# Cross attention of a decoder trunk: queries of two heads at a time by seven block products, with key and value tiles ahead of the probabilities in memory

## The chip, the cores and the metric

One core of a Trainium2 chip. The metric is the device time of one execution in microseconds; the time before is the median of three runs, and one execution was also taken by the hardware profiler. The engines are TensorE (PE in the profile, with its weight loads apart as PEld), VectorE (DVE), ScalarE (ACT), GpSimd (POOL) and SyncE (SP). SP issues the plain loads, POOL the loads that add to what is already there.

## The reference

Two decoder layers over 512 tokens of width 1024. Each layer is a half-step feed-forward, a token mixer (differential attention in layer 0, a pooling mixer in layer 1), cross attention to 256 memory tokens, and a second half-step feed-forward; after each stands a layer norm of the scaled sum. The change lies in the cross attention:

```python
def memory_cross_attention(x, mem, wq, wkv, wo):
    q = (x @ wq).reshape(B, S, XA_HEADS, XA_HEAD_DIM)
    k, v = jnp.split(mem @ wkv, 2, axis=-1)
    ...
    s = jnp.einsum('bshd,bmhd->bhsm', q, k).astype(jnp.float32) * (XA_HEAD_DIM ** -0.5)
    p = jax.nn.softmax(s, axis=-1).astype(v.dtype)
    o = jnp.einsum('bhsm,bmhd->bshd', p, v).reshape(B, S, D_MODEL)
    return o @ wo
```

## The kernel before

Every product is kept near float32 by splitting both factors into a high part (a cast to fp32r by ACT, line 120) and a low part (the rest, subtracted by DVE, line 121) and adding three matmuls, high by high, high by low and low by high (`mm3`, lines 205 to 207). Weights come from memory as raw tiles, and each 128x1024 block is split into the tiles `wh` and `wl`. The tokens stand in four tiles `X`; PE turns them (`pt`), and ACT and DVE split the turned blocks into `xh` and `xl` (`turn`).

The feed-forward stages already use seven block products in place of eight (a 2x2 scheme of blocks: the rows of X in two halves of 256 tokens, the weights in two halves of rows and of columns). `second_factors` makes the sums of token blocks that the scheme needs, and `up` loads weight blocks, adds further blocks onto them with POOL DMAs (`more`), and runs the products into three banks `x`, `y` and `z`. Cross attention does not use this before the change: `xa_main` takes each head's keys (`pk`, 48 matmuls of 256 columns), its values (`pv`, 48), and its queries (`xq`, 48 matmuls of 512 columns; for the first head of layer 1 in 96 of 256). Beside that, `weave` lets `xa_side` put in a piece of side work each time the main work has gained a set credit (2500): scores `xs`, softmax, turned probabilities, outputs `xo`. `to_tokens` then multiplies by wo and adds to X. In layer 1 the keys and values of the first two heads and the keys of the third run beside the pooling mixer (`early_kv`). Query, key and value weights are loaded in tiles of 1 MB for a head, two such raw tiles being there, and the splits use five `wh` and five `wl` tiles.

A scheduling layer writes one fixed order for each engine ahead of the run, and an engine takes its instructions in that order: an instruction that waits holds up all behind it on the same engine.

Of the kernel before, what the change touches and what calls it, by code (L numbers as in the profile page):

```python
# [9 lines left out]
F32 = mybir.dt.float32  # L10
# [7 lines left out]
P = 128  # L18
# [26 lines left out]
GATES = {"xa": (1, 2)}  # L45

# [63 lines left out]
class Trunk:  # L110
    def __init__(self, tc, a, out, upto=8):
        self.tc, self.nc, self.a, self.out, self.upto = tc, tc.nc, a, out, upto
        self.side, self.late, self.gates = [], [], []
        self.ln_next_gb, self.kv_bufs = None, 8
# [95 lines left out]
    def weave(self, main, side, gap, lead=0):  # L210
# [3 lines left out]
        for ns in main:  # L214
            self.clock += ns
# [44 lines left out]

    def raw_heads(self, w, c0):
# [21 lines left out]
    def wide(self, raw):  # L283

        got = []
        for j in range(0, 8, 4):
            t = self.hl([P, 4, 256])
            self.split_weights(t[0], t[1], raw[:, j : j + 4])
            got += [(t[0][:, i], t[1][:, i]) for i in range(4)]
        return got  # L290

    def rows(self, w, k0, kn, c0, homes=None):


        got = []
        for k in range(0, kn, 4):
            n = min(4, kn - k)
            raw = self.raw_tile((4, S))
            r0 = (k0 + k) * P
            self.nc.sync.dma_start(  # L300
                raw[:, :n], w[r0 : r0 + n * P, c0 : c0 + S].rearrange("(k p) n -> p k n", p=P)
            )
            if homes:
                got += [home() for home in homes]
                for j, t in enumerate(got):
# [151 lines left out]
    def turn(self, t, half, tag="px"):  # L457
# [6 lines left out]
        if self.ln_next == "ffn":  # L464
# [544 lines left out]
    def da_values(self, h, vs):  # L1009

        raw = self.raw_cols(self.a["da_w_qkv"][0], 2 * D + h * P)
        ws = self.wide(raw)
# [232 lines left out]
    def pool_mixer(self, layer, ln):  # L1245
# [37 lines left out]
        wg = self.wide(self.pool_w)  # L1283
        self.begin_ln(layer, ln, 1.0)
        for t in range(NT):
# [16 lines left out]
            self.turn_late()  # L1302
# [33 lines left out]
    def xa_kv(self, w, h):  # L1336
        kt = self.keys.pop(0) if self.keys else (yield from self.xa_k(w, h))
        return kt, (yield from self.xa_v(w, h))

    def xa_k(self, w, h, raw=None, then=None, turn=True):  # L1340
        rk = raw or self.raw_cols(w, h * 256)
        ps = self.mm("pk").rearrange("p (c n) -> p c n", c=2)
        for j in range(2):
            with self.after(self.x_split if raw and not then else ()):
                wk = self.cols(rk, j)
            if then and j == 1:
                then()
            for k in range(KC):
                yield self.mm3(
                    ps[:, j], (wk[0][:, k], wk[1][:, k]), self.memT[k], k == 0, k == KC - 1  # L1350
                )
        kt = self.kv_tiles((P, 2, MEM))
        if turn:
            self.turn_late()
# [8 lines left out]
    def xa_v(self, w, h, raw=None):  # L1363
        wv = self.wide(raw or self.raw_cols(w, D + h * 256))
# [10 lines left out]
    def xa_head(self, qs, kt, v):  # L1375
# [34 lines left out]
        for c in range(2):  # L1410
# [4 lines left out]
            o = self.pair("oT")  # L1415
            self.split(o[0], o[1], po)
            self.oT.append(o)
            yield

    def early_kv(self, layer, ln, heads, raws):  # L1420
        w, keys = self.a["xa_wkv"][layer], {}

        def load_more():
            keys[1] = self.raw_cols(w, 256)
# [7 lines left out]
        self.keys.append((yield from self.xa_k(w, heads, turn=False)))  # L1432
# [191 lines left out]
```

## Time and profile before

| | us |
|---|---|
| median of three runs | 1936.6 |
| lowest and highest run | 1935.6, 1938.74 |
| the profiled execution | 1932.35 |
| span of its trace | 1930.6 |
| cross attention, layer 0 (about) | 590 to 752 |
| cross attention, layer 1 (about) | 1460 to 1605 |

The span runs from the first to the last instruction of the profiled execution; the execution's own time lies 1.75 us above it and the median 4.25 above that. A line of the timeline gives the start, the duration, the engine, the line of the program, and what is written from what; in square brackets stands the idle time of the engine ahead of it and what ended it. A line of the table of stretches gives the stretch, its length, and the busy time with instruction count of PE, PEld, DVE, ACT and POOL, then the granted TensorE clock (1 is full), the share of the DMA engines, and GB/s. The groups of a tile give the number of instructions with minimum, median and maximum duration in ns, and the first and last start. The DMA list gives the number of loads, the size of each, and the median us from issue to landing.

### The profile page before, as it was taken

The numbers are of one execution on the slowest core, as the hardware profiler recorded it, in microseconds if no ns is written. First come the engines' busy times: TensorE is split into PE (matmuls) and PEld (weight loads), VectorE is DVE, ScalarE is ACT, GpSimd is POOL, SyncE is SP. The second block draws the span as 40 slices with busy tenths as digits, with TensorE's granted clock in tenths as the row PEclk, the third lists the DMA queues.
The fourth block names the chain that finished last, engine by engine and source line by source line (L and its number), as shares of the span: only waits on it lengthen the run. The fifth ranks groups of instructions, "written<-read, shape, count | busy, mean of one in ns | idle before, by whom it ended". The sixth has DMA issues, their size and how long they took to land.

```text
span 1930.6 us, 32520 instructions
## 1 busy us (share of the span) xinstructions
PE 1902.1 (99%) x13114; PEld 1740.5 (90%) x13114; DVE 1566.3 (81%) x2200; ACT 1022.2 (53%) x1580; POOL 315.0 (16%) x276
## 2 busy tenths in 40 slices
PE   8999999999999999999999999999999999999998
PEld 8999998888778888999998999999889889999997
DVE  7888889888867557888888988898887568988886
ACT  6555454567655435655554655455445436555553
POOL 2112121111210001211210321112040012111210
PEclk9999999999999999999999999999999999999999
DMA  9978772322134316977686587778244356867861
GB/s 239 220 169 182 175 138 77 90 80 74 48 117 142 110 66 186 186 175 164 139 194 179 104 179 168 177 162 185 89 153 134 115 140 120 181 158 170 183 133 56
DMA packets 246743, 277.96 MB, mean 144 GB/s; under 512 B 8256, under 2 KB 212544, under 8 KB 246592
## 3 DMA queue, kind: packets, MB, share of 16 engines
q0 software_dynamic: 92928, 92.29, 31.1%
q1 hardware_dynamic: 153664, 183.59, 29.2%
q8 instruction: 103, 1.69, 0.3%
q14 instruction: 48, 0.39, 0.1%
HBM read 273.75 MB, written 2.10 MB: 143 GB/s over the span
## 4 chain that ended last, share of the span: by engine, by line
PE 80%; DVE 12%; ACT 3%; DMA 2%; issue 2%; POOL 1%; SPq 1%; DVEq 0%; ACTq 0%; POOLq 0%
PE x L205 7%; PE x L206 7%; PE x L207 7%; PE z L206 4%; PE z L205 4%; PE z L207 4%; PE ps L205 4%; PE ps L207 4%; PE ps L206 4%; PE px L205 2%; PE px L207 2%; PE px L206 2%; DVE wl L121 2%; PE y L207 2%; PE x L681 2%
## 5 line engine op out<-in xcount | busy, mean ns | idle before, releaser
L666 POOL DMA_DIRECT2D ra<-in_ffn_w_in_dram x132 | 170.3, 1309 | 993.5 <-DVE wl L121 815.2
L120 ACT CAST wh<-ra 128x1024 fp32r<-128x1024 f32 x184 | 193.7, 1053 | 218.9 <-PE x L206 67.5
L121 DVE TENSOR_TENSOR wl<-ra,wh 128x1024 fp32r<-128x1024 f32 x184 | 223.8, 1220 | 73.0 <-ACT wh L120 72.5
L120 ACT CAST wh<-rc 128x1024 fp32r<-128x1024 f32 x136 | 143.1, 1053 | 118.6 <-PE x L206 43.1
L205 PE MATMUL x<-xe,wh 128*128 128x256 f32 x704 | 195.0, 277 | 0.0
L206 PE MATMUL x<-xe,wh 128*128 128x256 f32 x704 | 194.8, 277 | 0.0
L207 PE MATMUL x<-xe,wl 128*128 128x256 f32 x704 | 194.8, 277 | 0.0
L121 DVE TENSOR_TENSOR wl<-rc,wh 128x1024 fp32r<-128x1024 f32 x136 | 164.6, 1219 | 28.4 <-ACT wh L120 28.1
L120 ACT CAST wh<-b 128x1024 fp32r<-128x1024 f32 x112 | 117.8, 1052 | 131.3 <-PE x L206 67.7
L121 DVE TENSOR_TENSOR wl<-b,wh 128x1024 fp32r<-128x1024 f32 x112 | 136.7, 1220 | 40.2 <-ACT wh L120 40.2
L205 PE MATMUL x<-xh,wh 128*128 128x256 f32 x544 | 151.1, 278 | 0.0
L206 PE MATMUL x<-xl,wh 128*128 128x256 f32 x544 | 150.6, 277 | 0.0
L207 PE MATMUL x<-xh,wl 128*128 128x256 f32 x544 | 150.6, 277 | 0.0
L206 PEld LDWEIGHTS x<-xe,wh 128*128 128x128 f32 x704 | 132.5, 188 | 1.4
L205 PEld LDWEIGHTS x<-xe,wh 128*128 128x128 f32 x704 | 132.1, 188 | 1.3
L207 PEld LDWEIGHTS x<-xe,wl 128*128 128x128 f32 x704 | 132.2, 188 | 0.0
L121 DVE TENSOR_TENSOR wl<-raw,wh 128x1024 fp32r<-128x1024 f32 x64 | 81.8, 1285 | 38.8 <-ACT wh L120 38.2
L206 PEld LDWEIGHTS x<-xl,wh 128*128 128x128 f32 x544 | 102.5, 188 | 0.7
L205 PEld LDWEIGHTS x<-xh,wh 128*128 128x128 f32 x544 | 102.1, 188 | 0.7
L207 PEld LDWEIGHTS x<-xh,wl 128*128 128x128 f32 x544 | 102.1, 188 | 0.0
L207 PE MATMUL y<-xh,wl 128*128 128x256 f32 x352 | 98.4, 280 | 1.2
L206 PE MATMUL z<-xl,wh 128*128 128x256 f32 x352 | 97.5, 277 | 0.7 <-DVE xl L121 0.7
(429 smaller groups left out, 6291.6 us busy)
## 6 DMA issues: line engine op xcount, KB each, us to landing
ra<-in_ffn_w_in_dram POOLq DMA_DIRECT2D x132, 512.0 KB, 6.7
rc<-in_ffn_w_in_dram SPq DMA_DIRECT2D x88, 512.0 KB, 5.8
b<-in_ffn_w_out_dram SPq DMA_DIRECT2D x76, 512.0 KB, 4.8
ra<-in_ffn_w_in_dram SPq DMA_DIRECT2D x44, 512.0 KB, 5.4
rc<-in_ffn_w_in_dram POOLq DMA_DIRECT2D x44, 512.0 KB, 6.7
raw<-in_xa_wkv_dram SPq DMA_DIRECT2D x16, 1024.0 KB, 5.4
raw<-in_da_w_qkv_dram SPq DMA_DIRECT2D x16, 512.0 KB, 5.2
raw<-in_xa_wq_dram SPq DMA_DIRECT2D x8, 1024.0 KB, 4.9
```

Source lines behind the costliest of these rows:

```text
L120: self.nc.scalar.copy(hi, src),
L121: self.nc.vector.tensor_sub(lo, src, hi.bitcast(F32)),
L205: mm(out, w[0], x[0], start=start, stop=False, skip_group_check=again)
L206: mm(out, w[0], x[1], start=False, stop=False, skip_group_check=again)
L207: self.last_mm = mm(out, w[1], x[0], start=False, stop=stop, skip_group_check=again)
L666: nc.gpsimd.dma_start(t, source(*block), accum_op=ALU.add)
L681: self.last_mm = nc.tensor.matmul(ps[:, j], v[i][:, k, j * P : (j + 1) * P], x[l][:, k], start=n == i == l == 0, stop=n == 7 and i == 1, s ...
```

## The change

`xa_queries` takes the queries of two heads at once, 512 columns of wq, as seven block products of 24 matmuls with 256 columns each, in the order 0, 1, 3, 6, 4, 5, 2 of the scheme. Three of the seven weight operands are plain blocks, four are sums: four POOL DMAs per pair of heads add a block onto a raw tile once that tile's earlier contents have been split (`more`), sixteen in all. `xa_factors` makes the token sums: s1, a11, a12, s2, s4, s3 on DVE, and the splits of parts 3, 2, 6, 4 and 5 on ACT and DVE, from the turned tokens 2 and 3 after the layer norm. A table, `XA_ORDER`, sets the order of the pieces in each layer: a digit is a piece of that head's keys and values, `s` a step of the factors, `q` and `r` one product of the first and second pair of heads, `Q` and `R` the place from which the side work may use that pair. The side work now comes at a credit of 2100. The fourth weight block (`rd`) is loaded only after the third product's weights are split. Key, value and wo weights are loaded in halves of 512 KB into raw tiles of half the size (five in layer 0, four in layer 1), the `wh` and `wl` tiles become four, the key and value tiles lie in a pool ahead of the probabilities, and the pooling mixer no longer turns the last tokens itself.

```diff
+XA_ORDER = ("0000s00ss" "qq1q11qq1q11qQ" "r222r2r22rr3rrR33333", "qsqs2qsq2sq3qqQ" "r2r3rr33rrrR33")
...
+    def raw_quarter(self, w, r0, c0, width):
+        raw = self.raw_tile((4 * 256 // width, width))
+        rows = w[r0 : r0 + P * 4 * 256 // width, c0 : c0 + width]
+        self.last_load = self.nc.sync.dma_start(raw, rows.rearrange("(k p) n -> p k n", p=P))
+        return raw
+    def raw_keys(self, w, h):
+        return [self.raw_quarter(w, 0, h * 256 + j * P, P) for j in range(2)]
+    def raw_values(self, w, h):
+        return [self.raw_quarter(w, r, D + h * 256, 256) for r in (0, S)]
...
-        if self.ln_next == "ffn":
+        if self.ln_next != "da":
...
-            self.turn_late()
+            if t < NT - 1:
+                self.turn_late()
...
-    def xa_kv(self, w, h):
-        kt = self.keys.pop(0) if self.keys else (yield from self.xa_k(w, h))
-        return kt, (yield from self.xa_v(w, h))
-    def xa_k(self, w, h, raw=None, then=None, turn=True):
-        rk = raw or self.raw_cols(w, h * 256)
+    def xa_kv(self, w, h, turn=None):
+        kt = self.keys.pop(0) if self.keys else None
+        if not kt:
+            kt = yield from self.xa_k(w, h, turn=turn)
+            yield None
...
-            o = self.pair("oT")
-            self.split(o[0], o[1], po)
-            self.oT.append(o)
+            if c == 0:
+                o = self.pair("oT" if len(self.oT) < 4 else "xe", (P, 2, S))
+            self.split(o[0][:, c], o[1][:, c], po)
+            self.oT.append((o[0][:, c], o[1][:, c]))
...
+    def xa_factors(self):
+        nc, F, H = self.nc, self.factors, 2 * P
+        a11, a12, a21, s1 = (self.tmp("oT", (P, 4, H)) for i in range(4))
+        def part(i, x, o=slice(0, H)):
+            self.split(F[i][0][:, :, o], F[i][1][:, :, o], x)
+        for t in (2, 3):
+            o = slice(t % 2 * P, (t % 2 + 1) * P)
+            pts = []
+            for half in range(2):
+                pt = self.aux("pt", ("py", "yz")[half]).rearrange("p (c n) -> p c n", c=4)
+                c0 = half * S
+                with self.behind():
+                    self.transpose4(pt, [self.X[t][:, c0 + j * P : c0 + (j + 1) * P] for j in range(4)])
+                pts.append(pt)
+            nc.scalar.copy(a21[:, :, o], pts[0])
+            nc.vector.tensor_tensor(s1[:, :, o], pts[1], a21[:, :, o], ALU.subtract)
+            part(3, s1[:, :, o], o)
+            part(2, pts[1], o)
+            yield
+        for r, (hi, lo) in zip((a11, a12), F):
+            nc.vector.tensor_tensor(r, hi.bitcast(F32), lo.bitcast(F32), ALU.add)
+        s2, s4, s3 = s1, a12, a21
+        nc.vector.scalar_tensor_tensor(s2, s1, -1.0, a11, ALU.mult, ALU.subtract)
+        nc.vector.scalar_tensor_tensor(s4, s2, -1.0, a12, ALU.mult, ALU.subtract)
+        part(6, s4)
+        yield
+        part(4, s2)
+        nc.vector.tensor_tensor(s3, a11, a21, ALU.subtract)
+        part(5, s3)
+        yield
+    def xa_queries(self, w, h, q):
+        nc, H = self.nc, 2 * P
+        def source(row, col):
+            c0 = (h + col - 1) * H
+            return w[(row - 1) * S : row * S, c0 : c0 + H].rearrange("(k p) n -> p k n", p=P)
+        def load(*block):
+            t = self.raw_tile((4, H))
+            nc.sync.dma_start(t, source(*block))
+            return t
+        def more(t, *block):
+            nc.gpsimd.dma_start(t, source(*block), accum_op=ALU.add)
+        def operand(raw):
+            v = self.hl([P, 4, H])
+            self.split_weights(v[0], v[1], raw)
+            return v
+        def product(ps, v, a, start=False):
+            x = self.factors[a]
+            for j in range(2):
+                o = slice(j * P, (j + 1) * P)
+                for k in range(4):
+                    yield self.mm3(
+                        ps[:, j], (v[0][:, k, o], v[1][:, k, o]), (x[0][:, k], x[1][:, k]),
+                        start and j == k == 0, j == 1 and k == 3, True,
+                    )
+        bank = lambda t: t.rearrange("p (j n) -> p j n", j=2)
+        halves = slice(0, H), slice(H, S)
+        scale = (D // XA_H) ** -0.5
+        def done(i, half, src, by):
+            hi, lo = (t[:, :, halves[half]] for t in q[i])
+            self.split_scaled(hi, lo, src, by)
+        ra = load(1, 1)
+        x = bank(self.aux("x", "px"))
+        v = operand(ra)
+        more(ra, 1, 2)
+        rc = load(2, 1)
+        yield from product(x, v, 0, True)
+        p1 = self.tmp("p", (P, 2, H))
+        nc.scalar.copy(p1, x)
+        yield None
+        y = bank(self.aux("y", "yz"))
+        v = operand(rc)
+        yield from product(y, v, 1, True)
+        nc.vector.tensor_tensor(p1, y, p1, ALU.add)
+        q[0] = self.pair("q", (P, 2, S))
+        done(0, 0, p1, scale)
+        yield None
+        z = bank(self.aux("z", "yz"))
+        v = operand(ra)
+        rd = load(2, 2)
+        more(ra, 2, 2)
+        yield from product(z, v, 3, True)
+        p5 = self.tmp("p", (P, 2, H))
+        nc.scalar.copy(p5, z)
+        yield None
+        v = operand(rd)
+        more(rd, 1, 2)
+        yield from product(z, v, 6)
+        yield None
+        v = operand(ra)
+        more(ra, 2, 1)
+        yield from product(x, v, 4)
+        u2 = self.tmp("p", (P, 2, H))
+        q[1] = self.pair("q", (P, 2, S))
+        nc.scalar.copy(u2, x)
+        nc.vector.tensor_tensor(u2, z, u2, ALU.add)
+        done(1, 0, u2, -scale)
+        yield None
+        yield from product(x, operand(rd), 5)
+        nc.vector.tensor_tensor(p5, x, p5, ALU.add)
+        done(1, 1, p5, -scale)
+        yield None
+        yield from product(x, operand(ra), 2)
...
+        done(0, 1, x, scale)
...
-        early = len(self.kv)
-        for h in range(XA_H):
-            if h >= len(self.kv):
-                self.kv.append((yield from self.xa_kv(wkv, h)))
-            kt, v = self.kv[h]
-            raw = self.raw_cols(wq, h * 256)
-            qs = []
-            ws = [self.cols(raw, c) for c in range(2)]
-            ps = [self.mm("xq") for c in range(2)]
-            for p in ((0, 2 * P), (2 * P, S)) if self.late else ((0, S),):
-                for c in range(2):
-                    yield from self.project(ps[c], ws[c], (p,))
-                    self.turn_late(max(len(self.late) - 1, 0) if c == 0 else 0)
-            for c in range(2):
-                q = self.pair("q")
-                self.split_scaled(q[0], q[1], ps[c], (D // XA_H) ** -0.5)
-                qs.append(q)
-            self.heads.append((self.clock, (qs, kt, v)))
-            if 0 < early and h + early < XA_H:
-                self.kv.append((yield from self.xa_kv(wkv, h + early)))
+        self.late, second = [], self.xa_factors()
+        qs = [[None] * 2 for n in range(2)]
+        works = {n: self.xa_queries(wq, 2 * i, qs[i]) for i, n in enumerate("qr")}
+        works.update((str(h), self.xa_kv(wkv, h)) for h in range(1, XA_H))
+        works["0"] = self.xa_kv(wkv, 0, lambda: next(second))
+        for n in XA_ORDER[layer]:
+            if n == "s":
+                next(second)
+            elif n in "QR":
+                i = "QR".index(n)
+                for j in range(2):
+                    q = [(qs[i][j][0][:, c], qs[i][j][1][:, c]) for c in range(2)]
+                    self.heads.append((self.clock, 2 * i + j, q))
+            else:
+                yield from self.part(works[n])
...
-        bufs = dict(q=8, oT=10, gb=2)
+        bufs = dict(xe=6, q=4, oT=4)
+        self.raw_rows = 2
         if layer == 0:
             self.kv, self.keys = [], []
             mem = self.side_pool("mem")
-            with self.other_pools():
+            with self.stage_pools(4, dict(raw=5), ("wh", "wl", "raw", "kv")):
                 self.stage["mem"] = mem
-                with self.phase_pool(("gb", "gb"), "p", pT=6, p=4, kv=8, _x=0, **bufs):
-                    self.kvp = self.phase["kv"]
+                with self.phase_pool(("xe", "xe"), "p", p=4, pT=4, _x=0, **bufs):
+                    self.kvp = self.stage["kv"]
                     with self.tc.high_priority():
                         self.load_memory("p")
                     self.xa(layer, ln)
             self.close_side()
         else:
-            with self.later, self.phase_pool(("gb", "gb"), "p", _x=0, pT=6, p=4, **bufs):
+            with self.later, self.phase_pool(("xe", "xe"), "p", _x=0, pT=4, p=4, **bufs):
                 self.xa(layer, ln)
     def xa(self, layer, ln):
-        self.heads, self.oT = [], []
-        self.weave(self.xa_main(layer), self.xa_side(), 2500)
+        self.heads, self.oT, self.factors = [], [], self.factor_tiles()
+        self.weave(self.xa_main(layer), self.xa_side(), 2100)
...
-            self.later.enter_context(self.other_pools(("wh", "wl", "mem", "raw")))
+            self.later.enter_context(self.stage_pools(4, dict(raw=4), ("wh", "wl", "mem", "raw")))
```

Where the instructions now stand is shown at two places. The first is DVE at the start of cross attention in layer 0, before the change, from the last step of the layer norm (line 380) to the first head's weights (`xl` low part of the turned tokens, `wl` of weights, `kv` of keys or values):

```order
L380 SCALAR_TENSOR_TENSOR X_77<-X_77,rstd,v 128x1024
L121 TENSOR_TENSOR xl<-pt,xh 128x4x128 x2
L121 TENSOR_TENSOR kv<-pk,kv 128x512
L121 TENSOR_TENSOR xl<-pt,xh 128x4x128 x2
L121 TENSOR_TENSOR wl<-raw,wh 128x1024 x4
L121 TENSOR_TENSOR kv<-pv,kv 128x512
L121 TENSOR_TENSOR wl<-raw,wh 128x1024 x2
L126 SCALAR_TENSOR_TENSOR q<-xq,q 128x512
```

and after it, from the first wide sum, a11, on (`oT` are the tiles that hold the sums s1, a11, a12, s2, s3, s4; lines 1479 to 1491 are `xa_factors`; `wl_6988` is the second product's weight block):

```order
L1484 TENSOR_TENSOR oT_6836<-xh_6439,xl_6441 128x1024
L124 TENSOR_TENSOR xl_6442<-oT_6839,xh_6440 128x4x128
L124 TENSOR_TENSOR xl_6442<-pt_6845,xh_6440 128x4x128
L1479 TENSOR_TENSOR oT_6839<-pt_6900,oT_6838 128x4x128
L1484 TENSOR_TENSOR oT_6837<-xh_6439,xl_6441 128x1024
L124 TENSOR_TENSOR xl_6442<-oT_6839,xh_6440 128x4x128
L124 TENSOR_TENSOR xl_6442<-pt_6900,xh_6440 128x4x128
L124 TENSOR_TENSOR kv_6936<-pv_6870,kv_6935 128x512
L1486 SCALAR_TENSOR_TENSOR oT_6839<-oT_6839,oT_6836 128x1024
L1491 TENSOR_TENSOR oT_6838<-oT_6836,oT_6838 128x1024
L1487 SCALAR_TENSOR_TENSOR oT_6837<-oT_6839,oT_6837 128x1024
L124 TENSOR_TENSOR wl_6988<-raw_6958,wh_6987 128x1024
```

The second product's weights stand behind the build of the sums, and the two steps just ahead of these rows are a narrow sum and a key split.

The second place is ACT at the start of cross attention in layer 1, before the change, from the last turned tokens of the early part (`xh`) to the second head's values:

```order
L120 CAST xh_15929<-pt_16177 128x4x128
L120 CAST xh_15930<-pt_16184 128x4x128
L375 ACTIVATE var_16192<-var_16192 128x1
L120 CAST kv_16229<-pk_16096 128x512
L120 CAST wh_16395<-raw_16389 128x1024
L120 CAST xh_15929<-pt_16295 128x4x128
L120 CAST xh_15930<-pt_16302 128x4x128
L120 CAST wh_16481<-raw_16479 128x1024
L125 ACTIVATE q_16381<-xq_16269 128x512
L120 CAST wh_16485<-raw_16479 128x1024
```

and after it, from the cast of the first summed block to that of the next key weights (`raw_16486` and `raw_16634` are the query weight blocks that POOL adds onto, `raw_16763` key weights; `p_16520` holds the first product, `p_16661` the third):

```order
L123 CAST wh_16630<-raw_16486 128x1024
L1543 COPY p_16520<-x_16488 128x512
L123 CAST xh_16163<-oT_16525 128x4x128
L123 CAST xh_16163<-pt_16531 128x4x128
L123 CAST wh_16669<-raw_16634 128x1024
L1478 COPY oT_16524<-pt_16576 128x4x128
L128 ACTIVATE q_16572<-p_16520 128x2x256
L123 CAST xh_16163<-oT_16525 128x4x128
L123 CAST xh_16163<-pt_16581 128x4x128
L1558 COPY p_16661<-z_16629 128x512
L123 CAST wh_16727<-raw_16486 128x1024
L123 CAST wh_16768<-raw_16763 128x1024
```

Casts of summed weight blocks (`wh_16630`, `wh_16727`) now stand ahead of the copy of the first product, of casts of turned tokens, of key weights and of the factors. On POOL the DMAs that add the blocks stand in the same queue as the layer norm's last step there:

```order
L393 TENSOR_TENSOR rstd_16278<-var_16277,mhalf_82 128x1
L393 TENSOR_TENSOR rstd_16358<-var_16357,mhalf_82 128x1
L1511 DMA raw_16486<-in_xa_wq_dram 128x4x256
L393 TENSOR_TENSOR rstd_16414<-var_16413,mhalf_82 128x1
L1511 DMA raw_16486<-in_xa_wq_dram 128x4x256
L1511 DMA raw_16634<-in_xa_wq_dram 128x4x256
L1511 DMA raw_16486<-in_xa_wq_dram 128x4x256
```

The first of them stands ahead of the last tokens' `rstd`, where before the change POOL had no DMA in this stage.

More of the change, by code (lines that the diff above doesn't have):

```diff
@@ L214, in weave @@
         for ns in main:
+            ns = ns or 0
             self.clock += ns
@@ L285, in wide @@
         got = []
-        for j in range(0, 8, 4):
+        for half in raw:
             t = self.hl([P, 4, 256])
-            self.split_weights(t[0], t[1], raw[:, j : j + 4])
+            self.split_weights(t[0], t[1], half)
             got += [(t[0][:, i], t[1][:, i]) for i in range(4)]
@@ L1011, in da_values @@
         raw = self.raw_cols(self.a["da_w_qkv"][0], 2 * D + h * P)
-        ws = self.wide(raw)
+        ws = self.wide([raw[:, :4], raw[:, 4:]])
         for t in range(0, NT, 2):
@@ L1282, in pool_mixer @@
             yield
-        wg = self.wide(self.pool_w)
+        wg = self.wide([self.pool_w[:, :4], self.pool_w[:, 4:]])
         self.begin_ln(layer, ln, 1.0)
@@ L1363, in xa_v @@
     def xa_v(self, w, h, raw=None):
-        wv = self.wide(raw or self.raw_cols(w, D + h * 256))
+        wv = self.wide(raw or self.raw_values(w, h))
         ps = self.mm("pv").rearrange("p (m n) -> p m n", m=2)
@@ L1431, in early_kv @@
             self.kv.append((kt, (yield from self.xa_v(w, h, raws[1] if h == 0 else None))))
-        self.keys.append((yield from self.xa_k(w, heads, turn=False)))
+        self.keys.append((yield from self.xa_k(w, heads)))
+    def xa_factors(self):
[28 more added lines that the diff above has]
+        yield
```

43 lines of the change are left out of this document (28 added, 15 removed).

## The prediction

> **What bounds the kernel now.** I read the page first (busy shares and the chain that ended last), then the groups of the query products, the timeline of single matmuls, a table of stretches of the two cross-attention stages, and last the rows of VectorE (DVE), ScalarE (ACT) and the DMAs at the start of each stage.
>
> ```profile
> PE 1902.1 (99%) x13114; PEld 1740.5 (90%) x13114; DVE 1566.3 (81%) x2200; ACT 1022.2 (53%) x1580; POOL 315.0 (16%) x276
> PE 80%; DVE 12%; ACT 3%; DMA 2%; issue 2%; POOL 1%; SPq 1%; DVEq 0%; ACTq 0%; POOLq 0%
> ```
>
> TensorE (PE) is busy 99% of the span and carries 80% of the chain. A matmul taken away is a gain only as long as nothing makes PE wait; a wait put in is lost whole. DVE is at 81%, so the second question is where DVE has room.
>
> ```profile
> 590.00:610.00 20.00, 19.59 (x142) 17.94 (x143) 17.22 (x22) 10.24 (x17) 1.08 (x1) 1.00 0.54 167
> 610.00:630.00 20.00, 20.00 (x150) 18.77 (x149) 10.70 (x16) 9.59 (x17) 0.00 (x0) 1.00 0.56 175
> 690.00:710.00 20.00, 20.00 (x95) 16.51 (x94) 9.13 (x15) 6.05 (x12) 0.00 (x0) 1.00 0.29 103
> 1460.00:1480.00 20.00, 19.02 (x162) 18.33 (x161) 16.85 (x21) 11.38 (x18) 1.83 (x2) 1.00 0.58 189
> 1480.00:1500.00 20.00, 20.00 (x120) 17.39 (x119) 10.54 (x19) 10.60 (x21) 0.00 (x0) 1.00 0.47 155
> ```
>
> The columns are PE, its weight loads, DVE, ACT, POOL, granted clock, DMA share and GB/s, for the start and the inside of cross attention in layer 0 (from 590 us) and layer 1 (from 1460 us). Inside a stage PE is full and DVE works 9 to 11 of 20 us: there is room. In the first 20 us of either stage DVE already works 17, with the last layer norm, the splits of X and the first weights.
>
> **What is removed.** The query products leave and seven block products per two heads come.
>
> ```profile
> L205 PE MATMUL xq<-xh,wh x144: 276/394/507, 605.0 to 1543.3; 128*128 128x512 f32 x112, 128*128 128x256 f32 x32
> L206 PE MATMUL xq<-xl,wh x144: 276/394/400, 605.3 to 1543.6; 128*128 128x512 f32 x112, 128*128 128x256 f32 x32
> L207 PE MATMUL xq<-xh,wl x144: 276/394/400, 605.5 to 1543.9; 128*128 128x512 f32 x112, 128*128 128x256 f32 x32
> ```
>
> That is 336 matmuls of 512 columns and 96 of 256 (head 0 of layer 1 runs in halves). The durations overlap, so the price is the distance from start to start:
>
> ```profile
> 1519.62 0.39 PE L207 MATMUL xq<-xh,wl 128*128 128x512 f32 x1
> 1519.85 0.39 PE L205 MATMUL xq<-xh,wh 128*128 128x512 f32 x1
> ...
> 1464.55 0.28 PE L205 MATMUL xq<-xh,wh 128*128 128x256 f32 x1
> 1464.66 0.28 PE L206 MATMUL xq<-xl,wh 128*128 128x256 f32 x1
> 1464.77 0.28 PE L207 MATMUL xq<-xh,wl 128*128 128x256 f32 x1
> ```
>
> 0.233 us (the mean over longer runs of such rows) for 512 columns, 0.113 for 256. Before: 336 x 0.233 + 96 x 0.113 = 89.1 us. After: four pairs of heads x 7 products x 24 = 672 matmuls of 256 columns, 75.9 us. PE gains 13.2 us, 6.8 in layer 0 and 6.4 in layer 1, if it never waits. This is arithmetic on measured distances; I leave it no error.
>
> The Trainium skill (TensorE: Matmul & The Clock Gate, section "Wait — 56ns, not 53.3ns?") speaks against so much: start to start is the columns at 2.4 GHz plus a fixed 2.5 ns, 216 and 109 ns here, by which the smaller tiles would save only 9.6 us. The trace's 0.233 and 0.113 differ from it, and here 512 columns cost a little over twice 256; the trace is used.
>
> **What is added.** Six more weight splits a layer (14 blocks of 128x1024 for queries instead of 8), and the factor build: the sums s1 to s4, a11 and a12 and the splits of parts 3, 2, 6, 4, 5. From the rows
>
> ```profile
> 597.88 1.28 DVE L380 SCALAR_TENSOR_TENSOR X<-X,rstd,v 128x1024 f32<-128x1024 f32 x1
> 599.08 1.28 DVE L121 TENSOR_TENSOR xl<-pt,xh 128x512 fp32r<-128x512 f32 x2
> 600.28 0.68 DVE L121 TENSOR_TENSOR kv<-pk,kv 128x512 fp32r<-128x512 f32 x1
> 602.76 1.29 DVE L121 TENSOR_TENSOR xl<-pt,xh 128x512 fp32r<-128x512 f32 x2 [1.80 <-ACT xh L120]
> 603.97 4.62 DVE L121 TENSOR_TENSOR wl<-raw,wh 128x1024 fp32r<-128x1024 f32 x4
> ```
>
> one 128x512 step takes 0.60 us of DVE's time (599.08 to 600.28 for two) and one 128x1024 step 1.14 ((4.62 - 1.22) / 3). On DVE the six splits are 6.8 us. The build's eight wide steps (a11, a12, s2, s4, s3 and three splits) take 9.1 and its six narrow ones 3.6, against 2.4 for the four narrow splits it replaces: 10.3. With the six narrow adds and subtractions that combine the products (3.6) that is some 21 us a layer. Over a stage of 150 us at half load it vanishes; the rows at 690 show where. It does not vanish at the start, where it is bunched.
>
> *Layer 0.* The first product's weight block is split right after the last X row (done 600.2), so its matmuls can start near 605 as before. After that DVE does in order: six narrow steps of the build, two of key and value, five wide sums, then the second product's weights. 8 x 0.60 + 5 x 1.14 + 1.14 = 11.6 us, so these are ready at 611.8. PE has 24 matmuls (2.7 us) and six that need no low part (0.7), from 605.0: it arrives at 608.4 and waits 3.4 us. The third product's weights come behind three more factor splits, another 1.2. The rest of the chain costs 0 to 1.2. Together 4.6 to 5.8, of which I take 5.0. The order on DVE is fixed beforehand, so nothing can be drawn ahead into these waits; the low end is the first wait alone, 3.4, with key products covering the rest.
>
> *Layer 1.* Here ACT is the trap. Weight blocks are summed by POOL's accumulating DMAs in place, and each may be issued only when the split of the earlier contents is done.
>
> ```profile
> 1462.95 1.22 DVE L247 TENSOR_TENSOR wl<-raw,wh 128x1024 fp32r<-128x1024 f32 x1
> 1464.08 1.28 DVE L378 SCALAR_TENSOR_TENSOR X<-X,mean,gb 128x1024 f32<-128x1024 f32 x1
> 1466.48 1.27 DVE L380 SCALAR_TENSOR_TENSOR X<-X,rstd,gb 128x1024 f32<-128x1024 f32 x1
> ...
> 602.15 1.07 ACT L120 CAST xh<-pt 128x512 fp32r<-128x512 f32 x2
> 603.11 2.96 ACT L120 CAST wh<-raw 128x1024 fp32r<-128x1024 f32 x3
> ...
> ra<-in_ffn_w_in_dram POOLq DMA_DIRECT2D x132, 512.0 KB, 6.7
> raw<-in_xa_wq_dram SPq DMA_DIRECT2D x8, 1024.0 KB, 4.9
> ```
>
> The feed-forward stage's accumulating load of the same 512 KB lands 6.7 us after its issue; a plain load (here of twice the size) takes 4.9, the lower bound. The first split ends near 1464.2, so the summed block is there at 1470.9 (1469.1). In ACT's order its cast stands ahead of the copy of the first product, four casts of X and a weight cast. Behind it: cast 0.95, copy 0.5, two casts of X 1.0; then on DVE the last low part, the addition and the low part of the value weights, 0.6 + 0.6 + 1.14, with small waits between them: 1475.7. PE, with the first two products (48 matmuls), 13 matmuls of values and eight transposes to do from about 1465.1, stands at those value weights from 1472.6: 3.1 us lost (1.3 at the lower bound). The next accumulated block is released at 1478.1 and lands at 1484.8; behind its cast stand a key weight cast (ready 1486.8) and the casts of parts 6 and 4. PE arrives at the keys at 1483.2: 3.6 us (1.8), then about 2.0 more for the two parts. With 0.9 before the first product, 0.7 before the third and 0 to 3.5 where products reuse the x bank, the sum is 10.3 to 13.8. From it go the waits that the old start has, of which the first stands here, with an SP issue that is used further down:
>
> ```profile
> 1463.17 0.41 PE L489 MATMUL pt<-ident,X 128*128 128x128 f32 x2 [0.51 <-DVE X L380]
> ...
> 1469.51 0.38 SPq L233 DMA_DIRECT2D raw<-in_xa_wq_dram  x1
> ```
>
> From start to start this one costs 0.67 and one 4 us later 0.63, 1.3 us together (PE busy 19.02 of 20 in the stretch from 1460). At the lower bound of the DMA: 5.4. I take 9, with ends 5.4 and 12.5.
>
> *Clock.* The one long wait near this stage is followed by a slow stretch:
>
> ```profile
> 1434.02 0.28 PE L205 MATMUL ps<-wh,pooled 128*128 128x256 f32 x1
> 1437.42 0.58 PE L206 MATMUL ps<-wl,pooled 128*128 128x256 f32 x1 [3.11 <-DVE wl L121]
> ...
> 1437.40:1441.00 3.60, 3.58 (x17) 3.58 (x18) 3.60 (x5) 0.00 (x0) 0.00 (x0) 0.53 0.57 198
> ```
>
> After 3.1 us idle PE ran 3.4 us at half speed and lost 1.7 us more. The new waits are 3.4 in layer 0, 3.1 and 3.6 in layer 1. Each may or may not draw such a stretch: 0 to 5.1 us; I take one, 1.7. (The same page of the Trainium skill, section "What's actually happening", has the clock fall after an idle window of about 3.4 us on a free-running raster; the 3.4 us of half speed here agree.)
>
> *What costs nothing.* Loads in halves double the issues on SP, 0.38 us each, in a queue that is idle most of the time. Wider buffers for q and oT and the key and value tiles in another pool change addresses, not work. X is turned the same number of times. The second feed-forward stage's first blocks now share memory with key and value tiles, so their loads start only some 2 us before the stage ends; by the plain 4.9 us they land before the third product needs them, and if not, 2 us are lost: in the range, not in the sum.
>
> **The sum.** -13.2 + 5.0 + 9.0 + 1.7 = +2.5 us. The profiled execution took 1932.35 us (span 1930.6), so 1934.9 for such an execution; the median of the runs is 1936.6, 4.25 above it, so **1939** in runs like these. A measurement of this kernel tells about 0.2%, 3.9 us, from no change, and 1939 lies within it. The bounds give -13.2 + 3.4 + 5.4 + 0 = -4.4 and -13.2 + 5.8 + 12.5 + 5.1 = +10.2: 1932 to 1947.
>
> **The rivals.** *The gain comes through.* The 9 us of layer 1 hang on one fixed order of ACT behind a DMA. If the casts behind it find the block already there, because the release is earlier than I place it and PE has the remaining keys and values to do, only DVE's own backlog counts: 3.4 + 1.2 in layer 0, some 1.5 in layer 1. -13.2 + 6.1 = -7.1, 1929.5; with nothing lost, 1923. For it: inside the stage DVE and ACT are half idle, and PE holds full today with a start nearly as crowded. Against it: 16.85 of 20 us of DVE at that start, and 7 us more are put there.
>
> *The chain closes in both layers (slower).* Each summed block is split, released, summed again and cast before ACT may serve PE; where the landing exceeds 6.7 us by 1 or 2 (16 such DMAs beside weight loads at 150 to 190 GB/s), each of the early links in both layers adds it, and the waits pass what the clock forgives: -13.2 + 5.8 + 12.5 + 3.4 = +8.5, 1945. It decides from landings of about 8 us on. Against it: DMA share is only 0.3 to 0.6 here.
>
> *Small tiles do not run at 0.113.* By a fixed cost per matmul the gain would be 9.6 instead of 13.2 (216 and 109 ns a matmul): 1942.7. The 24-matmul runs of 256 columns in this very stage say no.
>
> **How the numbers follow.** Forecast (between -2.5 and +6.5 us): 0.46, of it 0.29 inside 0.2% and 0.17 above. Gain comes through: 0.33, of it 0.32 faster by over 0.2%. Chain closes: 0.18. Small tiles: 0.03. So faster 0.32, same 0.30, slower 0.38. The likeliest case alone is 1934 to 1943; cases of both signs hold much, so the range reaches to 1926 and 1946, which leaves out the best third of the gain case and the worst third of the chain case.
>
> **What would show it.** In layer 0 one PE wait of 3 to 4 us after the first product, put down to DVE's wl; in layer 1 two of about 3 us, put down to DVE wl and ACT wh, with ACT itself waiting for the DMA into a query weight block; one or more stretches at half clock within 4 us of them; and the groups x, y, z at 0.113 apart. I am wrong if PE stays full over both starts (then 1923 to 1930), if the block lands within 5 us, or if PE waits later in the stage for scores.

## The result, and the profile after

The changed kernel takes 1955.55 us (median of four runs, 1951.99 to 1958.24), the kernel before 1936.62 beside it: a ratio of 1.0099 with a 95% interval of 1.0081 to 1.0116, 18.9 us slower. The forecast was 1939, the range 1926 to 1946. The profiled execution after took 1957.83 us.

The page of the changed kernel, busy shares and chain:

```profile
span 1955.7 us, 33215 instructions
PE 1908.6 (98%) x13354; PEld 1759.2 (90%) x13354; DVE 1608.0 (82%) x2244; ACT 1048.0 (54%) x1614; POOL 338.7 (17%) x292
PE 75%; DVE 14%; ACT 4%; DMA 4%; issue 2%; POOL 1%; SPq 1%; DVEq 0%; ACTq 0%; POOLq 0%
```

PE's share of the chain fell from 80% to 75%; DMA, DVE and ACT took what it lost. The same stretches as before show where (columns as before: PE, weight loads, DVE, ACT, POOL, clock, DMA share, GB/s); the last four lines are the 3.4 us behind each of four waits:

```profile
590.00:610.00 20.00, 19.26 (x151) 17.86 (x150) 19.84 (x27) 14.50 (x25) 3.85 (x3) 1.00 0.51 126
610.00:630.00 20.00, 16.41 (x127) 16.21 (x126) 15.79 (x17) 8.39 (x11) 2.56 (x2) 0.91 0.45 107
630.00:650.00 20.00, 13.53 (x102) 13.13 (x101) 8.93 (x10) 8.12 (x10) 1.29 (x1) 0.83 0.76 164
1480.00:1500.00 20.00, 15.11 (x116) 14.73 (x115) 15.59 (x20) 9.05 (x15) 3.79 (x3) 0.91 0.48 109
1500.00:1520.00 20.00, 16.98 (x128) 16.25 (x127) 16.88 (x17) 10.96 (x13) 3.84 (x3) 0.91 0.79 158
616.70:620.10 3.40, 3.40 (x16) 3.40 (x17) 3.40 (x4) 1.79 (x2) 0.00 (x0) 0.53 0.64 188
644.00:647.40 3.40, 3.36 (x16) 3.37 (x17) 2.05 (x3) 0.63 (x1) 0.00 (x0) 0.52 0.43 134
1493.50:1496.90 3.40, 3.40 (x20) 3.40 (x18) 3.40 (x5) 1.66 (x4) 0.00 (x0) 0.53 0.22 62
1507.50:1510.90 3.40, 3.40 (x17) 3.40 (x17) 2.20 (x2) 1.86 (x2) 0.39 (x1) 0.51 1.06 146
```

In the first 20 us of layer 0's stage DVE is full (19.84). In the next 40 us PE is not: 16.41 and 13.53 of 20, at a clock of 0.91 and 0.83. The timeline of PE names the waits:

```profile
616.69 0.58 PE L210 MATMUL y<-xh,wl 128*128 128x256 f32 x1 [3.59 <-DVE wl L124]
...
644.04 0.58 PE L208 MATMUL x<-xe,wh 128*128 128x256 f32 x1 [5.75 <-ACT p L1569]
...
1493.10 0.63 PE L506 MATMUL pt<-ident,X 128*128 128x128 f32 x4 [4.37 <-DVE xl L124]
...
1505.27 0.38 PE L208 MATMUL pk<-mem0h,wh 128*128 128x256 f32 x1 [2.00 <-ACT wh L123]
```

The longest, 5.75 us, is read on ACT (lines from before and around it) and POOL:

```profile
634.55 1.05 ACT L123 CAST wh<-raw 128x1024 fp32r<-128x1024 f32 x1 [0.69 <-DMA raw<-in_xa_wq_dram]
642.45 1.04 ACT L123 CAST wh<-raw 128x1024 fp32r<-128x1024 f32 x1 [6.85 <-DMA raw<-in_xa_wq_dram]
643.40 0.58 ACT L1569 COPY p<-x 128x512 f32<-128x512 f32 x1
...
633.17 1.29 POOL L1511 DMA_DIRECT2D raw<-in_xa_wq_dram  x1 [5.58 <-DVE wl L124]
...
raw<-in_xa_wq_dram POOLq DMA_DIRECT2D x16, 512.0 KB, 6.3
```

PE may not start the sixth product before ACT has copied the fifth out of the bank (line 1569). That copy takes 0.58 us, and the fifth product's last matmul began at 635.29. It stands behind a cast of a weight block that the seventh product needs, and that cast waits for an accumulating load issued at 633.17. The cast began 9.3 us after the issue; the median from issue to landing is 6.3 for the sixteen.

Taking each matmul's distance to the next, less the shortest usual distance for its size (0.229, 0.113 and 0.109 us for 512, 256 and 128 columns), and sorting what is left, gives the account of the profiled executions. The first column runs from the first key matmul of layer 0's cross attention to the first `x` of layer 1's feed-forward, the second from the first `ps` of layer 1's mixer to the first `x` of the last feed-forward. Half clock is what was lost while the granted clock stood at 0.50.

| us, after less before | layer 0, cross attention and second feed-forward | layer 1, mixer and cross attention |
|---|---|---|
| matmuls at the shortest distance | -6.0 | -5.9 |
| waits over 0.4 us | +11.6 | +8.4 |
| half clock | +3.2 | +4.0 |
| distances up to 8% longer | +2.5 | 0.0 |
| rest | +0.7 | +0.9 |
| measured (parts rounded) | +12.0 | +7.5 |

The saved matmuls are there. Some 20 us of waits and 7 us at half clock bury them. The spans of the two traces differ by 25.1 us; of the 5.6 that stand in neither column, 3.7 lie in the first feed-forward stage, whose code is the same in both. They are the profiled run's own; the medians differ by 18.9.

### The profile page after: what moved, and what is told of

The parts are those of the page before. It is cut to its first block, busy times and chain, and to the rows that moved or that the text cites. A ratio compares the mean times of both kernels' runs of the same rounds, so it can differ in the third digit from the quotient of the medians.

```text
span 1955.7 us, 33215 instructions
## 1 busy us (share of the span) xinstructions
PE 1908.6 (98%) x13354; PEld 1759.2 (90%) x13354; DVE 1608.0 (82%) x2244; ACT 1048.0 (54%) x1614; POOL 338.7 (17%) x292
## 3 DMA queue, kind: packets, MB, share of 16 engines
q8 instruction: 105, 1.72, 0.4%
## 4 chain that ended last, share of the span: by engine, by line
PE 75%; DVE 14%; ACT 4%; DMA 4%; issue 2%; POOL 1%; SPq 1%; DVEq 0%; ACTq 0%; POOLq 0%
PE x L208 7%; PE x L209 7%; PE x L210 7%; PE z L210 4%; PE z L209 4%; PE z L208 4%; PE ps L210 4%; PE ps L208 4%; PE ps L209 4%; DVE wl L124 3%; PE px L208 2%; PE px L210 2%; PE px L209 2%; DMA raw<-in_xa_wq_dram 2%; PE y L210 2%
## 5 line engine op out<-in xcount | busy, mean ns | idle before, releaser
L208 PE MATMUL x<-xe,wh 128*128 128x256 f32 x768 | 214.6, 279 | 6.4 <-ACT p L1569 5.7
L210 PE MATMUL x<-xe,wl 128*128 128x256 f32 x768 | 213.8, 278 | 0.7 <-DVE wl L124 0.7
L209 PE MATMUL x<-xe,wh 128*128 128x256 f32 x768 | 213.9, 278 | 0.0
L208 PE MATMUL x<-xh,wh 128*128 128x256 f32 x608 | 169.6, 279 | 0.0
L210 PE MATMUL x<-xh,wl 128*128 128x256 f32 x608 | 168.9, 278 | 0.5 <-DVE wl L251 0.5
L209 PE MATMUL x<-xl,wh 128*128 128x256 f32 x608 | 168.9, 278 | 0.0
L208 PEld LDWEIGHTS x<-xe,wh 128*128 128x128 f32 x768 | 144.9, 189 | 8.4 <-ACT p L1569 6.2
L209 PEld LDWEIGHTS x<-xe,wh 128*128 128x128 f32 x768 | 145.4, 189 | 1.4
L210 PEld LDWEIGHTS x<-xe,wl 128*128 128x128 f32 x768 | 145.3, 189 | 0.9 <-DVE wl L124 0.9
L124 DVE TENSOR_TENSOR wl<-raw,wh 128x1024 fp32r<-128x1024 f32 x76 | 96.5, 1274 | 31.5 <-ACT wh L123 30.7
L210 PEld LDWEIGHTS x<-xh,wl 128*128 128x128 f32 x608 | 114.4, 188 | 0.7 <-DVE wl L251 0.7
L208 PE MATMUL z<-xh,wh 128*128 128x256 f32 x384 | 107.6, 280 | 1.7 <-ACT xh L123 0.9
```

The costliest lines, as they stand in the source:

```text
L124: self.nc.vector.tensor_sub(lo, src, hi.bitcast(F32)),
L208: mm(out, w[0], x[0], start=start, stop=False, skip_group_check=again)
L209: mm(out, w[0], x[1], start=False, stop=False, skip_group_check=again)
L210: self.last_mm = mm(out, w[1], x[0], start=False, stop=stop, skip_group_check=again)
```

## The experiments

Each time is the median, with the ratio to the kernel before, run on the same chip.

**The rest of the change alone.** The head-by-head projection of before is used for both layers, on the new pools, halved loads and four weight tiles. The edit also puts back the credit of 2500 and lets the mixer turn the last tokens as before, though the expectation says that the turned tokens of the change stay:

```diff
+PLAIN = (0, 1)
...
-        self.weave(self.xa_main(layer), self.xa_side(), 2100)
+        main = self.xa_main_plain if layer in PLAIN else self.xa_main
+        self.weave(main(layer), self.xa_side(), 2500 if layer in PLAIN else 2100)
```

> The queries of both layers are projected head by head with 512 columns again, as before the change; the halved loads, the four wh and wl tiles, the moved pools and the turned tokens of the change stay. Theory (the loss is made by the seven products' own waits, 12.9 us of new PE idle in layer 0 and 8.8 in layer 1, and the half-clock stretches behind them): the time comes back to the kernel before, 1933 to 1941. Rival (the rest of the change costs it, by fewer weight tiles and smaller loads): 1945 or more.

1938.09 us, 1.0007 (0.9998 to 1.0017). The moved pools, smaller loads and fewer tiles cost nothing that can be told (3.3 us at most, by the interval). The loss comes with the seven products and what was changed for them: the factors, the order table and the new credit, which no run takes apart from them.

**Layer 0 alone** (layer 1 as in the experiment above).

> Seven products in layer 0 only; layer 1 projects its queries head by head as before the change. Theory: the trace puts about 10 to 12 us of the loss into layer 0 with the start of the feed-forward stage behind it, and 7 to 8 into layer 1, so 1945 to 1949. Rival (layer 1's chain of summed weight blocks is the main loss, as predicted): 1941 or less.

1947.37 us, 1.0055 (1.0038 to 1.0072), 10.6 us over the kernel before. Taking off the 1.3 us that the run without seven products stood above it, layer 0 costs about 9 and layer 1 the other 8. Neither layer is the main one; the forecast had layer 0 gaining 1.8 us before its share of the clock (-6.8 and +5.0).

**Without accumulating loads.**

```diff
         def more(t, *block):
-            nc.gpsimd.dma_start(t, source(*block), accum_op=ALU.add)
+            pass
```

> The sixteen accumulating loads of query weights are left out, so that four of seven weight operands of a pair are not the sums; all splits, products and factor sums stay. Theory (the casts on ACT wait for summed blocks, and what stands behind them on ACT and DVE waits too): the waits of 5.9 us in layer 0 and of 4.5 and 3.6 in layer 1 go, with three of the four half-clock stretches (1.7 each): 1936 to 1942. Rival (VectorE's backlog by the sums makes the waits): they stay, 1949 or more.

1939.81 us, 1.0019 (1.0010 to 1.0029): 15.9 of the 18.9 us hang on these sixteen loads. The run takes away their landing, the waiting for it and their traffic together. What stays is mainly two waits that other work makes:

```profile
614.49 0.38 PE L210 MATMUL y<-xh,wl 128*128 128x256 f32 x1 [3.59 <-DVE wl L124]
...
1486.74 0.58 PE L208 MATMUL z<-xe,wh 128*128 128x256 f32 x1 [3.08 <-ACT xe L123]
```

The first is unchanged to the hundredth: DVE's backlog at the start of layer 0, no DMA. The second is the same in layer 1, where part 6 of the factors comes late; two shorter ones of 0.84 and 1.27 us, also for factors, follow it.

**The fourth block loaded early.**

```diff
-        rc = load(2, 1)
+        rc, rd = load(2, 1), load(2, 2)
```

> The fourth weight block is loaded right behind the second one instead of after the third product's split. Theory (layer 0's wait of 5.9 us hangs on that late load: load, split, accumulating load, split, one after the other): it shrinks to 1 or less and its half-clock stretch goes, 1947 to 1950. Rival (the accumulating load is late because of the loads beside it on the queues): the wait stays, 1953 or more.

1953.15 us, 1.0084 (1.0069 to 1.0099), against 1.0099: the theory fell. Layer 0's wait stayed (6.04 us beyond the usual distance from start to start, 5.91 before). The plain load had been in time. The program text puts it behind the third product's split, but in the trace of the changed kernel SP had issued it before that split began (at 611.46 on ACT):

```profile
602.78 0.37 SPq L1507 DMA_DIRECT2D raw<-in_xa_wq_dram  x1
```

It is the third sum on the first tile that is late. That is what the rival said would be seen; its reason, other loads on the queues, was not tried. In layer 1 the wait on the turned tokens did shrink in this trace, from 4.54 us to 2.23, but the two intervals overlap.

**Order on ACT and DVE.** Casts and low parts of later weight blocks are queued behind the copies and factor splits traced ahead of them:

```diff
         z = bank(self.aux("z", "yz"))
-        v = operand(ra)
+        with self.after((c1,) + tuple(self.part_split)):
+            v = operand(ra)
...
-        v = operand(ra)
+        with self.after((c5,) + tuple(self.part_split)):
+            v = operand(ra)
         more(ra, 2, 1)
...
-        yield from product(x, operand(ra), 2)
+        with self.after((c2,)):
+            v = operand(ra)
+        yield from product(x, v, 2)
```

> The casts and low parts of the summed weight blocks are queued behind the copy that frees a bank and behind the casts of the factors; nothing else. Theory (instructions that PE needs stand on ACT and DVE behind a wait for an accumulating load): layer 0's wait of 5.9 us before the sixth product shrinks to under 1.5, layer 1's of 4.5 goes, and with them two or three half-clock stretches of 1.7: 1938 to 1944. Rival (the summed blocks themselves come too late, whatever the order): the waits move to the products that use these blocks, 1951 or more.

1950.46 us, 1.0081 (1.0065 to 1.0097); about 4 us better, a quarter to a third of what was expected. ACT's rows in layer 0 show the copy free, and the load as late as before:

```profile
632.65 0.59 ACT L1571 COPY p<-x 128x512 f32<-128x512 f32 x1 [0.88 <-PE x L210]
639.52 1.05 ACT L123 CAST wh<-raw 128x1024 fp32r<-128x1024 f32 x1 [6.28 <-DMA raw<-in_xa_wq_dram]
```

The sixth product no longer waits; the seventh, which needs the block, now does (2.24 us beyond the usual distance, where the sixth had 5.91):

```profile
643.17 0.36 PE L208 MATMUL x<-xh,wh 128*128 128x256 f32 x1 [2.08 <-DVE p L1576]
```

What ended this wait last is DVE's read of the x bank (line 1576), and on DVE that read stands behind the late block's low part, which began at 640.60. In layer 1 the turned tokens no longer wait, and the factors do:

```profile
1493.07 0.38 PE L208 MATMUL z<-xe,wh 128*128 128x256 f32 x1 [2.83 <-ACT xe L123]
1494.33 0.58 PE L209 MATMUL z<-xe,wh 128*128 128x256 f32 x1 [0.88 <-DVE xe L124]
```

Both readings were half right: the order costs, and behind it stands the next wait.

**The factor sums later in layer 0.**

```diff
-XA_ORDER = ("0000s00ss" "qq1q11qq1q11qQ" ...
+XA_ORDER = ("0000s00qqs1qs11qq1q11qQ" ...
```

> Only layer 0's table changes: the weights of the first two products are split before the wide sums of the factors. Theory (the 3.75 us wait of layer 0's second product is VectorE's backlog): it goes, with its half-clock stretch, 1949 to 1951.5. Rival (the backlog only moves to the third product and the fourth, which need the same sums): 1954 or more.

1950.05 us, 1.0071 (1.0054 to 1.0088). The 3.75 us wait is gone. On DVE the second product's weights now stand ahead of the sums:

```profile
603.25 0.68 DVE L124 TENSOR_TENSOR kv<-pk,kv 128x512 fp32r<-128x512 f32 x1
603.85 1.22 DVE L124 TENSOR_TENSOR wl<-raw,wh 128x1024 fp32r<-128x1024 f32 x1
...
606.78 1.22 DVE L1484 TENSOR_TENSOR oT<-xh,xl 128x1024 f32<-128x1024 f32 x1
```

**Both edits.**

> Both edits together. If the two causes add: 1932 to 1938, about the kernel before or a little faster. If taking away one wait only uncovers the other: 1940 or more.

1944.79 us, 1.0045 (1.0030 to 1.0060). The savings add (4.1 and 4.5 alone, 9.8 together by the differences to the kernel before), but the order of the casts brought less than forecast, so that the time lies in the range given for waits that uncover each other. Most of what is left sits in layer 1.

**Layer 1's covering work moved ahead.** First one key piece, then values and two key pieces:

```diff
-"qsqs2qsq2sq3qqQ" "r2r3rr33rrrR33"
+"qsqs2qsq2s3qqqQ" "r2r3rr33rrrR33"
...
+"qsqs22q3s3sqqqqQ" "r2r3rr333rrrR"
```

> Both edits, and in layer 1 the last head's first key weights stand ahead of the product that needs the twice summed block. If the keys' weights on ACT behind that block make the last wait of 2 to 4 us there: 3 to 5 us faster than with both edits alone, 1928 to 1934. If PE then waits for the factors instead: equal to both within 1.5 us.

1943.83 us, 1.0039 (1.0024 to 1.0054): equal within a microsecond, as for factors that are late.

> Both edits, and in layer 1 the third head's values and the last head's first two key pieces are put ahead of the products that need parts 6, 4 and 5 of the factors (the side work comes at a credit of 1700 there). Theory (layer 1's remaining waits of 7 us are VectorE's backlog by the factor sums, which only other matmuls can cover): 5 to 7 us less than with both edits, 1936 to 1940. Rival (the chain of accumulating loads sets it): the waits move behind the covered ones, 1942 or more.

1941.05 us, 1.0029 (1.0018 to 1.0040), 3 to 5 us better than with both edits (by the ratios and by the medians), less than the 5 to 7 forecast and between the two ranges. The wait for the factors shrank to 0.9 us; then the chain of loads takes over:

```profile
1503.17 0.28 PE L210 MATMUL x<-xe,wl 128*128 128x256 f32 x1
1505.71 0.38 PE L208 MATMUL x<-xh,wh 128*128 128x256 f32 x1 [2.26 <-ACT wh L123]
```

**The same, without accumulating loads, and with the early fourth block.**

> The kernel with all three order edits (factor sums later in layer 0, casts of later blocks behind what PE needs, layer 1's keys and values earlier), and the sixteen accumulating loads left out, so that four of seven weight operands of a pair are not the sums. Theory (only the chain of accumulating loads is left in the way; the matmuls saved are worth 13.2 us): 1924 to 1931. Rival (the saved matmuls are not worth that, since the 256-column products run at a longer distance or the rest of the change costs): 1933 or more.

1933.45 us, 0.9986 (0.9977 to 0.9995): faster than the kernel before, but by 2.9 us, not by 13. The rival's figure was met, not its reason. In the trace the saved matmuls are all there. Layer 0's two stages, bounded as in the account above, took 486.1 us against 489.4 before, with 2.3 us of waits against 1.4. Layer 1's mixer and cross attention came out where they were (232.5 against 232.7), with 9.3 us of waits against 5.0, and with the clock at 0.50 for 6.8 us instead of 3.4.

> All three order edits, and the fourth weight block loaded right behind the second one. Theory (layer 1's remaining waits of 5 us hang on the accumulating loads, of which the early fourth block frees one): 2 to 3 us less than without it, 1937 to 1940, about the kernel before. Rival (the third link on the first tile sets the end anyway): 1940 to 1943, unchanged.

1947.59 us, 1.0053 (1.0040 to 1.0066): about 6 us worse. With four raw tiles the early block takes the place of value weights, and ACT waits for those:

```profile
1473.01 0.59 ACT L1543 COPY p<-x 128x512 f32<-128x512 f32 x1
1477.98 1.04 ACT L123 CAST wh<-raw 128x1024 fp32r<-128x1024 f32 x1 [4.39 <-DMA raw<-in_xa_wkv_dram]
```

**Layer 0 alone, with both edits.**

> Seven products in layer 0 alone, with both edits of order; layer 1 projects its queries head by head. Layer 0's stage took 3 us less than before in the trace with both edits, the start of the next stage 1 to 3 more. Theory (what is left of the loss sits in layer 1): 1933 to 1937, within 0.2% of the kernel before. Rival (the new pools and the next stage's start take the gain back): 1938 to 1941.

1937.19 us, 1.0004 (0.9995 to 1.0013): the time of the kernel before, and 0.2 us above the range of the theory.

The last run moves a key piece of the third head ahead of the seventh product:

```diff
-"0000s00qqs1qs11qq1q11qQ" "r222r2r22rr3rrR33333"
+"0000s00qqs1qs11qq1q112qQ" "r22r2r22rr3rrR33333"
```

> Seven products in layer 0 alone, with both order edits, and one key piece of the third head put ahead of the last product; layer 1 projects its queries head by head. Theory (layer 0's last wait of 2 us is the third accumulating load, which 24 matmuls cover): 2 to 3 us less than without the moved piece, 1933 to 1935.5, faster than the kernel before by 1 to 3. Rival (what layer 0 saves is given back at the start of the next stage whatever the waits): 1936.5 to 1938, as without it.

1933.62 us beside 1935.04, 0.9994 (0.9985 to 1.0003). The wait ahead of the seventh product is gone from the trace, and the two stages of layer 0 took 487.5 us against 489.4. Whether this version beats the kernel before is not settled: its interval reaches 1.

## Why the prediction was wrong

*What bounds the kernel, and the saved matmuls.* Right. Counted in the trace, 336 matmuls of 512 columns went and 576 of 256 came net, worth 13.2 us at 0.233 and 0.113; at the shortest distances, as in the account, 11.9.

*Layer 0's first wait.* Right in place, cause and size: 3.4 us forecast, 3.59 idle found, put down to DVE's `wl`; the two runs on order and loads show the cause.

*Layer 0, "the rest of the chain costs 0 to 1.2".* This step failed. In its place stood a wait of 5.9 us with a half-clock stretch behind it, and one of 0.9 ahead of it; a further 1.4 us came later in the stage, on the turned probabilities at 690. The prediction walked layer 1's casts behind accumulating loads one by one and called ACT the trap there, but passed over the same order in layer 0: the copy that frees the x bank behind the cast of a block whose third summand had just been issued. The forecast had 6.7 us for a landing; here the cast began 9.3 us after the issue, while SP issued three weight loads between 633.9 and 636.9. By these rows the order alone would have cost some 3 us: with a landing after 6.7 us the copy would have ended near 641.5 (an estimate), and PE's last matmul before the wait began at 638.01. What made this landing late was not tried.

*Layer 1.* Right in kind and near in size: 9 us net forecast, 7.5 in cross attention's own waits (8.8 less the old 1.3). The wait on the keys behind the second summed block is there (2.2 us, 3.6 forecast), and so are those for two parts behind it (1.4, 2.0 forecast). The place of the first wait was off. It fell on the turned tokens: their bank is freed by a low part on DVE whose cast on ACT stands behind the cast of the first summed block, and that block landed 7.8 us after its issue.

```profile
1481.69 1.31 POOL L1511 DMA_DIRECT2D raw<-in_xa_wq_dram  x1 [2.95 <-DVE wl L251]
1489.58 1.04 ACT L123 CAST wh<-raw 128x1024 fp32r<-128x1024 f32 x1 [4.29 <-DMA raw<-in_xa_wq_dram]
1491.53 0.59 ACT L123 CAST xh<-pt 128x512 fp32r<-128x512 f32 x1
1492.27 0.68 DVE L124 TENSOR_TENSOR xl<-pt,xh 128x512 fp32r<-128x512 f32 x1
```

*The clock.* The other term that was far too small: one half-clock stretch was taken of three that were thought possible, and four were found in cross attention, 6.4 us instead of 1.7. Three of the waits that drew one were of 3.6 to 5.75 us; the fourth was 2.00, 0.45 and 0.56 with single matmuls between.

*The rival that came nearest* is the chain closing in both layers, at 1945 with a chance of 0.18. Its picture was right: waits behind summed blocks in both layers. Its condition was not: of the sixteen landings only two took 8 us or more (8.1 and 9.2), and the wait on the keys in layer 1 stood behind one of 5.6. It was priced with the same 0 to 1.2 in layer 0, and so stopped 10 us short; the upper end of the range stood on it.

*What else was said.* The pools and the halved loads cost nothing that can be told, as said. The next stage's start was held up by 1.0 to 1.2 us (0.8 before) in this and all later kernels with the new pools, within the 2 that were allowed.

## What to carry to other kernels

On engines that work in order, look at what stands behind each instruction that waits for a DMA: a copy of half a microsecond that frees a bank kept PE waiting 5.9 us here, and taking it out from there won back only 3.7 of them, since the next wait stood behind it. Walk every stage of the change with the same care, not the one that looks worst, and price a long wait of TensorE with its half-clock stretch. Fewer matmuls pay only if the operands that they need can be made in time: here 12 us of matmuls were bought with loads, sums and splits that the start of each stage could not hold.

## What the runs showed of the hardware

PE ran at half clock for 3.2 to 3.4 us (0.51 to 0.53 in the windows shown) behind all four long waits in cross attention; in the second the clock already stood at 0.50 from 642 to 644, before PE resumed. The Trainium skill (TensorE: Matmul & The Clock Gate, section "What's actually happening") has the clock fall after an idle window of about 3.4 us, and the window free-running, 3413 ns long. The length agrees, though in the fourth case the clock fell behind a wait of 2.00 us and two short ones, with a few matmuls between them. One shorter wait is enough at times: ahead of the seventh product 2.08 us idle drew a stretch with the casts queued later (0.50 from 643.7 to 647.0), while 1.72 us with both edits and 1.95 with layer 0 alone drew none.

Unexpected were two steady distances between matmuls of 256 columns at full clock. The changed kernel in its second feed-forward stage, then the kernel before in the same stage (start, duration):

```profile
799.79 0.28 PE L209 MATMUL z<-xe,wh 128*128 128x256 f32 x1
...
800.85 0.28 PE L209 MATMUL z<-xe,wh 128*128 128x256 f32 x1
```

```profile
799.82 0.28 PE L207 MATMUL x<-xe,wl 128*128 128x256 f32 x1
...
800.50 0.28 PE L207 MATMUL x<-xe,wl 128*128 128x256 f32 x1
```

Nine distances in 1.06 us are 0.118 each, six in 0.68 are 0.113. The longer one held for some 380 matmuls after the wait at that stage's start, which cost 1.7 us. In the first stage of the profiled execution it held for some 780 and cost 3.3; a half-clock stretch there cost 1.6, and smaller parts bring the sum to that stage's 3.7. Executions of the variants fall into either without a change in code at that place. By its size it can be part of the scatter of some us between runs, which no run shows by itself; what starts and ends it was not tried.
